# Linear attention on one core: stores of octets 0 to 7 cut into four transfers each

## The chip, the core and the metric

The kernel runs on one core of a Trainium2 chip. The metric is the device time of one execution in microseconds (us). The core has TensorE (PE, with its weight loads PEld), VectorE (DVE), ScalarE (ACT), GpSimd (POOL), SyncE (SP) and 16 DMA engines, which carry all transfers between HBM (the chip's main memory) and SBUF (the on-chip memory of 128 partitions, called rows here).

## The reference

Q, K and V have the shape batch 8, heads 12, sequence 512, dim 64 in fp32, so there are 96 heads.

```python
Q_feat = np.maximum(0, Q)
K_feat = np.maximum(0, K)
KV = np.einsum('bhkd,bhkv->bhdv', K_feat, V)
K_sum = np.sum(K_feat, axis=2)
numerator = np.einsum('bhqd,bhdv->bhqv', Q_feat, KV)
denominator = np.einsum('bhqd,bhd->bhq', Q_feat, K_sum)
return (numerator / (denominator[:, :, :, None] + 1e-10)).astype(np.float32)
```

Each input and the output have 12.58 MB.

## The kernel before

The 96 heads are worked in 12 octets of 8 heads (`NO` is 12), and K and V of an octet in two groups of 4 heads. All loads are issued ahead, in the order K, V, Q of octet 1, then of octet 2 and so on (lines 94 and 106). They come from GpSimd, because its transfers turn fp32 into bf16 on the way, and each waits for a free buffer: six octets of K and V, seven of Q. K and V of octet 0 come as fp32 through the SyncE and ScalarE queues (`k_first`, `v_first`).

For each octet the kernel prepares K (`kf`, line 138: ReLU and a mask) and V (`vo`, lines 140, 145 and 147), multiplies them on TensorE into `ps_kv` (line 152), copies the sums out to `kvd` (line 162), transposes Q (line 173) with ReLU (line 181), forms the numerator `ps_ot` (line 203) and the denominator (lines 212 to 224), transposes back (line 230) and multiplies with the reciprocal into `o_sb` (line 236). `o_sb` holds an octet's output as 128 rows of 32 x 64 fp32, 8 KB a row; a row is contiguous in the output as well, and the rows follow each other there. `outp` has `DELAY + 2` = 8 such buffers, and `k_first` and `v_first` use two of them at the start.

`store(o, o_sb)` issues the store from SyncE's queue (line 249), in octet order. The schedule is written out by hand, and a store of octet 0 to 5 also waits until the load of K of the octet six later (`k_load[o + DELAY]`) has landed; a store of a later octet waits only for its data and for what stands ahead of it in SyncE's queue. The last octet is stored in two halves of the columns (line 247). The program that comes out counts the completions of SyncE's and ScalarE's transfers on eight semaphores in turn, and a transfer waits for the earlier use of its semaphore.

Of the kernel before, what the change touches and what calls it, by code (L numbers as in the profile page):

```python
# [10 lines left out]
def kernel(  # L11
# [7 lines left out]
    nc = tc.nc  # L19
    B, H, S, D = Q.shape  # L20
    assert D == 64
    P = 128
# [5 lines left out]
    RQ = S * 8 // P  # L28
# [3 lines left out]
    NO = NG // 2  # L32
    assert NO * 8 == NH and R == 16 and RQ == 32
    DELAY = 6

    fp32 = mybir.dt.float32
    bf16 = mybir.dt.bfloat16
# [3 lines left out]
    def pool(name, bufs, **kw):  # L41
        return ctx.enter_context(tc.tile_pool(name=name, bufs=bufs, **kw))
# [6 lines left out]
    rcp = pool("rcp", 2)  # L49
    outp = pool("outp", DELAY + 2)  # L50
    otp = pool("otp", 2)
# [37 lines left out]
    k_load = {}  # L89
    after_load = mybir.DependencyInfo(mybir.DependencyClass.Sync, mybir.DependencyReason.DATA)  # L90
# [151 lines left out]
    def store(o, o_sb):  # L242
        Ov = Or[o].rearrange("p (r d) -> p r d", d=D)
        if o == NO - 1:
            for j in range(2):
                rs = slice(RQ // 2 * j, RQ // 2 * (j + 1))
                nc.sync.dma_start(out=Ov[:, rs], in_=o_sb[:, rs])
            return
        st = nc.sync.dma_start(out=Ov, in_=o_sb)
        if o + DELAY < NO:  # L250
            tc.add_manual_dep(st.ins, k_load[o + DELAY].ins.name, after_load, reason="store after load")

    def out_tile():
        return outp.tile([P, RQ, D], fp32, name="o_sb", tag="o_sb")
# [19 lines left out]
    def backs(o):  # L274
        o_sb = out_tile()
        for j in range(2):
            norm(o, j, back(o, j), o_sb)
        store(o, o_sb)
# [26 lines left out]
    o = NO - 2  # L305
# [10 lines left out]
    o_sb = out_tile()  # L316
# [4 lines left out]
    for i in range(2):  # L321
        relu_q(o + 1, i, transp(o + 1, i), nc.vector if i == 1 else None)
    norm(o, 1, ps, o_sb)
    store(o, o_sb)
    idle(5, o + 1)
    out_t(o + 1, (0,))
# [32 lines left out]
```

## Time and profile before

| what | value |
|---|---|
| time, median of 2 runs | 126.88 us (126.72 to 127.03) |
| profiled execution | 127.0 us, span 125.2 us |
| PE, DVE, ACT, POOL busy | 85.0, 81.0, 79.0, 23.7 us |
| HBM read, written | 37.75 MB, 12.58 MB |
| transfers into `out_dram` from `o_sb` | 11 of 1024 KB, 8.9 us from issue to landing (median); 2 of 512 KB, 4.5 us |
| loads of K, V and Q | 512 KB as they land, 20.5 to 21.8 us from issue to landing |
| mean granted TensorE clock | 0.950 |

The span runs from the first to the last instruction of the profiled execution; what is in its time beside the span is 1.8 us. Busy time is summed over the whole span, while the stages differ: loads alone at first, then loads and stores, then stores alone. In the view of DMA slices a digit is the busy share of the 16 DMA engines in a fortieth of the span. The bytes of a load are counted as they land, in bf16, half of what is read from HBM.

### The profile page before, as it was taken

The page shows a single profiled execution, that of the slowest core. Times are in us where ns is not written, and L with a number is a line of the kernel's source. Part 1 is how long each engine was busy: PE and PEld are TensorE (multiplying, and loading weights), DVE is VectorE, ACT ScalarE, POOL GpSimd, SP SyncE. Part 2 cuts the span into 40 slices and gives each one's busy share as a digit, 9 for nine tenths or more (in the row PEclk, how much of TensorE's full clock was granted, in tenths as well). Part 3 has the DMA queues.
Part 4 walks back from the last instruction along what each step waited for, and adds up shares of the span by engine and source line. Part 5 has one row for each costly group of instructions (what it writes and reads, how often), then busy time and mean ns, then how long its engine had stood idle before and what let it go on. Part 6 is the DMA issues. An engine that isn't in the chain of part 4 may idle for free.

```text
span 125.2 us, 2614 instructions
## 1 busy us (share of the span) xinstructions
PE 85.0 (68%) x1067; PEld 76.9 (61%) x1067; DVE 81.0 (65%) x176; ACT 79.0 (63%) x114; POOL 23.7 (19%) x40
## 2 busy tenths in 40 slices
PE   0000547898989979898966985955997597797600
PEld 0000547796878879787855983943975595775500
DVE  2006963679889797979859349449549409978610
ACT  0003737999899898989877576845499095547000
POOL 6922124221242213322121130210000000000000
PEclk9999999999999999999999599996899869999996
DMA  3999999999999999999999999999999999999991
GB/s 92 365 306 229 215 209 211 213 211 217 207 217 208 211 213 211 214 273 311 214 247 341 210 222 342 234 217 325 258 215 305 279 215 307 425 419 419 432 403 73
DMA packets 10139, 32.66 MB, mean 261 GB/s; under 512 B 784, under 2 KB 784, under 8 KB 8720
## 3 DMA queue, kind: packets, MB, share of 16 engines
q0 software_dynamic: 7712, 17.83, 74.1%
q1 hardware_dynamic: 2144, 13.63, 27.1%
q10 hardware_dynamic: 272, 1.05, 2.2%
q8 instruction: 8, 0.13, 0.4%
q14 instruction: 3, 0.02, 0.0%
HBM read 37.75 MB, written 12.58 MB: 402 GB/s over the span
## 4 chain that ended last, share of the span: by engine, by line
DVE 37%; DMA 28%; PE 19%; ACT 7%; issue 3%; DVEq 1%; ACTq 0%
DMA v_sb<-in_V_dram 20%; DVE o_sb L236 15%; PE ps_kv L152 10%; DMA k_first<-in_K_dram 7%; DVE kf L138 7%; PE ps_bk L230 7%; DVE vo L140 4%; ACT kvd L162 3%; DVE vo L147 3%; DVE den L220 2%; PE ps_qt L173 2%; DVE rec L224 2%; DVE own L215 2%; ACT qt L181 2%; ACT vo L145 1%
## 5 line engine op out<-in xcount | busy, mean ns | idle before, releaser
L152 PE MATMUL ps_kv<-vo,kf 128*128 128x132 bf16 x384 | 30.2, 240 | 19.9 <-ACT vo L145 13.8
L152 PEld LDWEIGHTS <-kf 128*128 128x128 bf16 x384 | 27.4, 107 | 21.6 <-DVE vo L140 12.9
L236 DVE TENSOR_TENSOR o_sb<-ps_bk,rec 128x1024 f32<-128x1024 f32 x24 | 28.3, 1219 | 13.6 <-PE ps_bk L230 13.6
L162 ACT CAST kvd<-ps_kv 64x260 bf16<-64x260 f32 (+1 forms) x54 | 18.6, 345 | 16.6 <-PE ps_kv L152 13.9
L205 ACT COPY ot_sb<-ps_ot 128x1024 f32<-128x1024 f32 x24 | 24.1, 1013 | 6.8 <-PE ps_ot L203 5.9
L230 PE MATMUL ps_bk<-ident,ot_sb 128*128 128x128 f32 x192 | 23.4, 276 | 0.4 <-ACT ot_sb L205 0.4
L181 ACT ACTIVATE qt<-ps_qt 128x1024 bf16<-128x1024 bf16 x23 | 22.4, 1028 | 0.2
L230 PEld LDWEIGHTS ps_bk<-ident,ot_sb 128*128 128x128 f32 x192 | 21.2, 143 | 0.7 <-ACT ot_sb L205 0.7
L203 PE MATMUL ps_ot<-qt,kvd 128*128 128x256 bf16 x96 | 14.9, 283 | 9.9 <-DVE o_sb L236 9.0
L138 DVE TENSOR_SCALAR kf<-k_sb,mask 128x1024 bf16<-128x1024 bf16 x44 | 18.4, 459 | 4.5 <-DMA k_sb<-in_K_dram 4.5
L203 PEld LDWEIGHTS <-kvd 128*128 128x128 bf16 x96 | 9.2, 100 | 13.2 <-issue 11.0
L173 PE MATMUL ps_qt<-ident,q_sb 128*128 128x128 bf16 x192 | 14.7, 237 | 0.7 <-DMA q_sb<-in_Q_dram 0.7
L173 PEld LDWEIGHTS <-q_sb 128*128 128x128 bf16 x192 | 13.3, 108 | 1.4 <-DMA q_sb<-in_Q_dram 1.3
L140 DVE TENSOR_SCALAR vo<-v_sb,mask 128x1024 bf16<-128x1024 bf16 x22 | 11.0, 501 | 4.7 <-DMA v_sb<-in_V_dram 4.7
L145 ACT ACTIVATE vo<-v_sb,mask 128x1024 bf16<-128x1024 bf16 x10 | 11.5, 1154 | 2.0 <-DMA v_sb<-in_V_dram 1.8
L94 POOL DMA_DIRECT2D v_sb<-in_V_dram x11 | 8.2, 750 | 22.2 <-DMA q_sb<-in_Q_dram 9.4
L106 POOL DMA_DIRECT2D q_sb<-in_Q_dram x12 | 7.1, 588 | 20.9 <-DMA k_sb<-in_K_dram 15.3
L94 POOL DMA_DIRECT2D k_sb<-in_K_dram x11 | 7.9, 717 | 15.4 <-DMA v_sb<-in_V_dram 9.8
L212 PEld LDWEIGHTS <-qt 128*128 128x128 bf16 x192 | 6.8, 96 | 3.6 <-ACT qt L181 2.5
L212 PE MATMUL ps_den<-kvd,qt 128*128 128x16 bf16 x192 | 7.3, 180 | 1.9 <-ACT qt L181 1.7
L145 ACT ACT_TABLE_LOAD x1 | 1.3, 1283 | 11.3 <-DMA v_first<-in_V_dram 11.3
L138 DVE TENSOR_SCALAR kf<-k_first,mask 128x1024 bf16<-128x1024 f32 x4 | 2.8, 750 | 7.7 <-DMA k_first<-in_K_dram 7.7
(24 smaller groups left out, 31.8 us busy)
## 6 DMA issues: line engine op xcount, KB each, us to landing
out_dram<-o_sb SPq DMA_DIRECT2D x11, 1024.0 KB, 8.9
q_sb<-in_Q_dram POOLq DMA_DIRECT2D x12, 512.0 KB, 20.7
k_sb<-in_K_dram POOLq DMA_DIRECT2D x11, 512.0 KB, 21.8
v_sb<-in_V_dram POOLq DMA_DIRECT2D x11, 512.0 KB, 20.5
k_first<-in_K_dram SPq DMA_DIRECT2D x1, 1024.0 KB, 9.3
v_first<-in_V_dram ACTq DMA_DIRECT2D x1, 1024.0 KB, 10.5
out_dram<-o_sb SPq DMA_DIRECT2D x2, 512.0 KB, 4.5
```

Source lines behind the costliest of these rows:

```text
L94: ld = eng.dma_start(out=t.rearrange("p g r d -> p g (r d)"), in_=X[2 * o:2 * o + 2].rearrange("g p f -> p g f"))
L138: nc.vector.tensor_scalar(kf[g][:, :, s, :], k_sb[g], scalar1=0.0, scalar2=mask[:, 0, s:s + 1], op0=Alu.max, op1=Alu.mult)
L140: nc.vector.tensor_scalar(vo[g % NB][:, :, 0, 2:D + 2], v_sb[g], scalar1=mask[:, 1, 0:1], scalar2=None, op0=Alu.mult)
L152: nc.tensor.matmul(ps_kv[:, g % 2, 0:2 * (D + 2)].rearrange("p (t d) -> p t d", t=2), kf[g][:, r, :, :].rearrange("p s d -> p (s d)"), vo[ ...
L162: copy(kvd[o % NK][64 * c:64 * c + 64, 4 * gs.start + s:4 * gs.stop:2, c * D1:c * D1 + D1].rearrange("p (g t) d -> p g t d", t=2), ps_kv[6 ...
L173: nc.tensor.transpose(ps[:, u, :], q_sb[o][:, i * (U // 2) + u, :], ident)
L181: nc.scalar.activation(to, ps, Act.Relu)
L203: nc.tensor.matmul(ps[:, i], kvd[o % NK][:, h, 1:2 * D + 1], q[:, :, h, :], start=True, stop=True, skip_group_check=True)
L205: nc.scalar.copy(ot[o][:, :, 4 * j:4 * j + 4], ps.rearrange("p h u c -> p u h c"))
L212: nc.tensor.matmul(ps[:, u], qt_sb[o % NZ][:, u, :], kvd[o % NK][:, :, 0:2 * D1:2 * D1 - 1], start=True, stop=True, skip_group_check=True)
L230: nc.tensor.transpose(ps[:, 2 * v:2 * v + 2].rearrange("p c d -> p (c d)"), ot[o][:, 8 * j + v].rearrange("p h c -> p (h c)"), ident32)
L236: nc.vector.tensor_tensor(o_sb[:, rs], ps, rec[o][:, rs].unsqueeze(2).to_broadcast([P, 16, D]), op=Alu.mult)
```

## The change

The stores of octets 0 to 7 go out in four transfers each: rows 0 to 111 in full; the right halves (4 KB) of rows 112 to 127; the left halves of the first n of these 16 rows; and the left halves of the other 16 - n. n is another number for each octet (`FIRST`). Each of the four has the same dependence on the load of K six octets later as the whole store had. Octets 8 to 11 are stored as before. What is computed and the order of all instructions on the other queues stay as they were.

```diff
+    FIRST = {0: 8, 1: 12, 2: 14, 3: 10, 4: 15, 5: 13, 6: 11, 7: 9}
...
-        st = nc.sync.dma_start(out=Ov, in_=o_sb)
-        if o + DELAY < NO:
-            tc.add_manual_dep(st.ins, k_load[o + DELAY].ins.name, after_load, reason="store after load")
+        half, a, full = RQ // 2, 112, slice(0, RQ)
+        n = FIRST.get(o)
+        if n is None:
+            parts = [(0, P, full)]
+        else:
+            parts = [(0, a, full), (a, P, slice(half, RQ)), (a, a + n, slice(0, half)), (a + n, P, slice(0, half))]
+        for lo, hi, rs in parts:
+            st = nc.sync.dma_start(out=Ov[lo:hi, rs], in_=o_sb[lo:hi, rs])
+            if o + DELAY < NO:
+                tc.add_manual_dep(st.ins, k_load[o + DELAY].ins.name, after_load, reason="store after load")
```

## The prediction

> **What bounds the kernel now.** I read the page first: the slices of the DMA engines, the queues and the HBM line.
>
> ```profile
> DMA  3999999999999999999999999999999999999991
> GB/s 92 365 306 229 215 209 211 213 211 217 207 217 208 211 213 211 214 273 311 214 247 341 210 222 342 234 217 325 258 215 305 279 215 307 425 419 419 432 403 73
> ...
> q0 software_dynamic: 7712, 17.83, 74.1%
> q1 hardware_dynamic: 2144, 13.63, 27.1%
> ...
> HBM read 37.75 MB, written 12.58 MB: 402 GB/s over the span
> ```
>
> The 16 DMA engines are busy from the second slice to the end. GB/s counts what lands: a load reads fp32 and lands bf16, so 213 is 426 on the reading side, the same as the 425 of the stores at the end. HBM moves 37.75 + 12.58 = 50.33 MB; at 425 GB/s that is 118.4 us of a 125.2 us span. No compute engine is above 68%. Second, stretches of the span:
>
> ```profile
> 10.00:50.00 40.00, 30.89 (x408) 28.64 (x409) 31.48 (x70) 33.34 (x50) 10.48 (x16) 1.00 1.10 213
> ...
> 80.00:100.00 20.00, 14.49 (x175) 12.67 (x173) 12.37 (x24) 11.47 (x17) 0.56 (x1) 0.89 1.08 263
> 100.00:107.00 7.00, 5.63 (x58) 5.12 (x57) 3.82 (x6) 5.22 (x8) 0.00 (x0) 0.82 1.08 272
> 107.00:118.00 11.00, 9.50 (x115) 8.38 (x114) 8.47 (x17) 4.87 (x10) 0.00 (x0) 1.00 1.01 425
> ```
>
> The columns are the stretch, its length, the busy time of PE, PEld, DVE, ACT and POOL, the clock, the DMA share (last but one) and GB/s. The share is 1.0 or more in every stage: loads alone until 50, loads mixed with one store per 10 us until 101, stores alone after 107. The store rate of 425 GB/s makes 1 MB 2.47 us; on 16 engines each moves 8 rows of 8 KB, 0.307 us a row and 0.154 us a half row. Third, SyncE's waits and its issues:
>
> ```profile
> SPq L249 <- DMA k_sb<-in_K_dram: 98.5, 6, 50.5
> SPq L249 <- DVE o_sb L236: 10.0, 2, 8.1
> ```
> ```profile
> 91.52 0.33 SPq L249 DMA_DIRECT2D out_dram<-o_sb  x1
> 101.75 1.86 SPq L249 DMA_DIRECT2D out_dram<-o_sb  x4
> 105.56 0.33 SPq L249 DMA_DIRECT2D out_dram<-o_sb  x1
> 114.11 0.33 SPq L249 DMA_DIRECT2D out_dram<-o_sb  x1
> 118.23 1.46 SPq L247 DMA_DIRECT2D out_dram<-o_sb  x2
> ```
>
> SyncE mostly waits, and at 101.75 it issues the stores of octets 5 to 8 at once. From there the backlog of stores never runs out: the completion records of octet 10's store (issued at 114.11) start between 119.30 and 120.65 us on the different engines, after the last store's first half was issued at 118.23. The last half completes between 121.97 and 123.55 us, mean 122.65; 1.65 us later the span ends. So the end is the slowest DMA engine's total work. The compute chain runs parallel to it from 84 us on, with about 1 us to spare at 118.23; it catches up if the DMA is relieved by more.
>
> **The change part by part.** Eight stores of one transfer become four each: 24 transfers more, the same bytes.
>
> *Issues on SyncE.* 24 x 0.333 us (an issue in the timeline) = 8.0 us of SyncE. Octets 0 to 4 are issued 10 us apart, so it costs nothing there; for octets 5 to 7 four issues take 1.33 us while one store keeps the engines busy for 2.47 us. I take 0. Without that cover it would be 3 x 3 x 0.333 = 3.0 us.
>
> *New waits on SyncE.* The changed program counts hardware transfers on eight semaphores in turn, so a transfer waits for the one eight before it. With four to a store that is the same part of the store two octets earlier. Octet 7's 112 rows wait for octet 5's, octet 8's store for octet 6's 112 rows; everything later in SyncE's order (8 to 11) queues behind. Before, these four went out together. A completion is seen some 0.37 us after its record (k_first's last record 9.67, the waiting kf at 10.04), and from issue to data it is 1.26 us (118.23 issued, first completion 120.72 less 1.23 of data): 1.63 us. Meanwhile the store in between holds the engines for 2.47 us, and the slowest are never dry. Cost 0; with the cover gone 1.63 us twice, 3.3 us. What VectorE awaits of old stores before it writes o_sb 8 to 11 had landed some 30 us earlier: 0.
>
> *Completion packets.* Each transfer writes one 4-byte completion per engine that it uses; the records show 22 ns for most. An engine in all 24 added transfers pays 0.53 us, one in only the eight right-half transfers 0.18. I take 0.35.
>
> *Uneven shares.* The 112 rows are 7 per engine and the right halves one per engine. The left halves go out as n and 16 - n rows, one row to an engine, so some engines get two and others none. If the same engines come first each time, one gets 16 left halves in place of 8 and one gets none: +1.23 to -1.23 us (8 x 0.154). If the favoured engines change from transfer to transfer it is about 0. The gain is bounded by how far the slowest engine is from the mean: 123.55 - 122.65 = 0.9 us. Between -0.9 and +1.23 I take the middle, +0.15.
>
> [...]
>
> *Other rows under each engine.* In the trace every large transfer spans 128 rows, eight to an engine, and at that all stages run at 425 GB/s: no row shows an engine waiting for another on the way out of SBUF. The 112-row transfer gives an engine seven rows, so its rows are no longer the eight that loads and stores share now, and the three small transfers have all 16 engines read within 16 neighbouring rows at one time. Lower end: an engine's rate does not depend on the row, 0 (a gain is excluded, since an engine already moves at its full rate). Upper end: each row waits for one other engine's row, 2.47 us per octet more, 19.7 in all. The nearest rows are the full-rate stores, so I stay near the lower end: one row time lost among the seven long rows, since blocks of 7 shift against blocks of 8 by at most that, and half of one among the half rows. 1.5 x 0.307 = 0.46 us per octet, 3.7 us for eight. Loads between the store's packets hide some of it in octets 0 to 4; nothing does in octets 5 to 7.
>
> [...]
>
> *Sum.* Profiled execution 127.0 us = span 125.2 + 1.8 around it; + 0.35 + 0.15 + 3.7 = 131.2 us. The two timed runs have the median 126.88, 0.1 below the profiled one; I forecast **131.1 us**. With half a row time lost per octet (1.2) and 0.2 for the rest it is 128.4; with three row times (7.4) and 1.2 it is 135.6: the likeliest case's own range.
>
> **Rivals.** *The rows don't matter* (the other side). An engine reads any row at 0.307 us; then only completions and unevenness are left: 127.0 + 0.5 = 127.5 us. For it: the full rate in stages of very different mixes, and a cost that no row of the trace shows. Against it: every one of those rows has the same eight rows per engine. It decides as soon as the loss is under 0.31 us per octet (2.5 us, 2%, over eight).
>
> *The slow engines are the relieved ones.* The shares level the 1.58 us between first and last engine: at best 0.9 us off, 126.1 us. For it: the spread exists, in two clusters; between 107.03 and 107.55 nine engines complete octet 5's store, and seven between 108.17 and 108.78. Seven 16 KB instruction packets lie before that, at about 27, 37, 48, 58, 71, 83 and 98 us, which looks like one engine each. Against it: nothing tells which engine numbers they are, and 7 late engines cannot all be the most relieved.
>
> *Full collision.* Each row waits for another: + 19.7 us, 147 us. Against: engines drift apart by 1.6 us, five row times, and so do not stay in step.
>
> *The new semaphore waits run dry.* The two waits cost 1.63 us each, 130.8 us with the small terms; it decides if a store lands over 0.8 us later than its 2.47 us. For it: they sit where no load fills in. Against: the slowest engines are behind.
>
> **How the numbers follow.** Lost row times 0.46 (0.42 of it beyond 2%, 0.04 within); full collision 0.06; waits 0.04; rows don't matter 0.26, all within 2%; levelled 0.18, 0.15 within and 0.03 for a gain beyond what I can price. Slower by over 2% (about what a measurement of this kernel can tell from no change) 0.52, within 0.45, faster 0.03. The range of 126.2 to 135.6 leaves out the full collision (0.06), the best of the levelled case (0.07) and the top of the likeliest (0.06).
>
> **What would show it.** Right: in the mixed stretches the DMA share stays at 1.0 or more while GB/s over the store's slices falls below the 340s; in the stretch of octets 5 to 7 GB/s is under 400; store packets take longer than the 0.31 us of now; loads land later. Wrong: the store-only stretch still shows about 425 GB/s and the last load lands at 107.6 us, as now. Levelling would show as completions of the last store within less than 1 us. Dry engines would show as DMA slices under 9 near 109 and 112 us.

## The result and the profile after

The changed kernel takes 128.5 us (median of 128.45 and 128.54), before 126.88 us: ratio 1.0121, 95% interval 1.0091 to 1.0151. The profiled execution has a span of 126.7 us against 125.2. It is slower, but by 1.6 us where 4.2 were forecast.

The same stretches as before; the last two columns are the DMA share and GB/s:

```profile
10.00:50.00 40.00, 30.73 (x385) 28.30 (x385) 30.45 (x69) 31.89 (x45) 10.50 (x16) 1.00 1.10 212
...
80.00:100.00 20.00, 14.62 (x183) 13.29 (x182) 12.36 (x24) 11.70 (x17) 0.56 (x1) 0.93 1.09 263
100.00:107.00 7.00, 5.76 (x63) 5.23 (x61) 3.69 (x6) 5.10 (x8) 0.00 (x0) 0.84 1.08 264
107.00:118.00 11.00, 9.50 (x115) 8.38 (x114) 8.46 (x17) 5.00 (x10) 0.00 (x0) 1.00 0.94 375
```

Up to 100 us the rate has not changed: 263 GB/s from 80 to 100 as before, although split stores lie there. From 107 to 118 us, where stores run alone, 425 GB/s have become 375 and the share has fallen from 1.01 to 0.94. Cut finer, the kernel before and then the changed one:

```profile
108.00:112.00 4.00, 4.00 (x56) 3.93 (x54) 3.28 (x8) 1.67 (x7) 0.00 (x0) 1.00 1.02 428
112.00:116.00 4.00, 2.85 (x35) 2.04 (x34) 3.24 (x6) 2.97 (x3) 0.00 (x0) 1.00 1.01 422
116.00:120.00 4.00, 1.82 (x16) 1.58 (x15) 2.36 (x2) 0.00 (x0) 0.00 (x0) 1.00 1.00 420
```
```profile
108.00:112.00 4.00, 4.00 (x57) 3.94 (x55) 3.30 (x8) 1.57 (x6) 0.00 (x0) 1.00 1.00 387
112.00:116.00 4.00, 2.85 (x36) 2.03 (x34) 3.31 (x6) 3.07 (x4) 0.00 (x0) 1.00 0.86 342
116.00:120.00 4.00, 1.95 (x16) 1.71 (x16) 2.35 (x2) 0.00 (x0) 0.00 (x0) 1.00 1.02 424
```

Two different things are to be seen. From 108 to 112 us the engines are busy all the time (1.00) and yet move only 387 GB/s in place of 428: packets take longer. In the trace's DMA records between 107.6 and 118 us, 18 of 426 packets of 8 KB take over 1.3 times the median of 0.31 us, up to 0.87 us; before it was 1 of 537. From 112 to 116 us engines also stand idle (0.86). From 116 us, with the whole stores of octets 8 to 11, all is as before.

The idle time has to do with SyncE's issues. The timeline of SyncE in the changed kernel, start and duration; from the second line on these are the last three transfers of octet 6, then octet 7's four, then octet 8's store:

```profile
103.45 0.32 SPq L258 DMA_DIRECT2D out_dram<-o_sb  x1
103.82 1.44 SPq L258 DMA_DIRECT2D out_dram<-o_sb  x1
105.30 0.99 SPq L258 DMA_DIRECT2D out_dram<-o_sb  x1
106.34 0.61 SPq L258 DMA_DIRECT2D out_dram<-o_sb  x1
108.95 0.32 SPq L258 DMA_DIRECT2D out_dram<-o_sb  x1
109.32 1.20 SPq L258 DMA_DIRECT2D out_dram<-o_sb  x1
110.56 1.38 SPq L258 DMA_DIRECT2D out_dram<-o_sb  x1
111.98 0.98 SPq L258 DMA_DIRECT2D out_dram<-o_sb  x1
113.06 0.36 SPq L258 DMA_DIRECT2D out_dram<-o_sb  x1
```

Before, the four issues in a row from 101.75 us took 0.33 to 0.44 us each. Here the first five of octets 5 and 6 (101.78 to 103.45 us) take 0.29 to 0.43, the sixth 1.44: SyncE is held, by what no record shows. The gap before 108.95 is octet 7's wait for octet 5's 112 rows, 1.9 us in the view of SyncE's waits. Octet 8's store, issued at 103.18 us before the change, now goes out at 113.06, and engines are dry (without work) before its data come.

The DMA records give the loss of the mean engine, whose last completion moved by 1.5 us, from 122.70 to 124.17. The idle time is 0.15 of 4 us, 0.6 us. What packets from 107 us on took beyond the median of their size comes to 0.6 us an engine, 0.1 before: 0.5 us more. Completion records of SyncE's queue take 0.48 us an engine over the whole run, 0.21 before. The three add up to about 1.4 us.

So four causes stood side by side: the other rows under each engine, if they are what makes packets longer (theory R; the texts below also speak of collisions or of engines that wait for each other, which no record shows as such), semaphore waits (W or S), held issues (H) and uneven shares (U). The last are in the records: followed from packet to packet, one engine takes three half rows for each of octets 5 to 7 (from 108.02 to 113.59 us), and another a single one for octet 6 (at 110.13) and for octet 7 (at 112.69). The experiments take the four apart. Each edit below is to the list `parts` of the changed kernel; an octet not named is stored whole. Times are medians, ratios against the kernel before on the same chip.

### The profile page after: what moved, and what is told of

The parts are those of the page before. It is cut to its first block, busy times and chain, and to the rows that moved or that the text cites. A ratio compares the mean times of both kernels' runs of the same rounds, so it can differ in the third digit from the quotient of the medians.

```text
span 126.7 us, 2646 instructions
## 1 busy us (share of the span) xinstructions
PE 85.3 (67%) x1067; PEld 77.7 (61%) x1067; DVE 81.3 (64%) x176; ACT 79.2 (63%) x114; POOL 23.3 (18%) x40
## 4 chain that ended last, share of the span: by engine, by line
DVE 35%; DMA 28%; PE 23%; ACT 5%; issue 2%; DVEq 1%; ACTq 0%
DMA v_sb<-in_V_dram 21%; DVE o_sb L238 15%; PE ps_kv L154 11%; DMA k_first<-in_K_dram 8%; PE ps_bk L232 6%; DVE kf L140 6%; DVE vo L142 4%; PE ps_qt L175 3%; ACT kvd L164 2%; DVE vo L149 2%; DVE den L222 2%; PE ps_ot L205 2%; DVE rec L226 2%; DVE own L217 2%; ACT qt L183 2%
## 5 line engine op out<-in xcount | busy, mean ns | idle before, releaser
L175 PE MATMUL ps_qt<-ident,q_sb 128*128 128x128 bf16 x192 | 15.7, 247 | 0.4 <-DMA q_sb<-in_Q_dram 0.4
L175 PEld LDWEIGHTS <-q_sb 128*128 128x128 bf16 x192 | 14.3, 113 | 0.9 <-DMA q_sb<-in_Q_dram 0.6
```

Of the source, the lines that this page charges most:

```text
L175: nc.tensor.transpose(ps[:, u, :], q_sb[o][:, i * (U // 2) + u, :], ident)
```

## Experiments: which octets, shares and waits cost

**e1: octets 0 to 4 alone.**

```diff
-        n = FIRST.get(o)
+        n = FIRST.get(o) if o < 5 else None
```

> Only octets 0 to 4 go out in four transfers; octets 5 to 11 go out whole, so that no store at the end waits for the one two octets earlier. Theory W (the new semaphore waits run the DMA engines dry): no slice of the DMA share under 0.95 between 107 and 118 us, time 126.3 to 127.3 us, no slower than before. Theory U (the engine that always gets two left halves has too much work): five eighths of its excess stay, about +0.9 us, 127.6 to 128.0 us, with one engine last. Theory R (other rows under each engine cost time, as forecast): five octets of eight, 127.5 us or more, with slower stores before 100 us.

Measured: 127.11 us, ratio 1.0006 (0.9998 to 1.0015). Five of the eight splits cost nothing that can be told. R as I had priced it, the same for each octet, falls here, and so does U at its full price.

**e2: the whole excess early.** (9 and 11 stand for n in octets 4 and 3.)

```diff
+        SHARE = {0: (8, 12), 1: (14, 10), 2: (15, 13), 3: (11, 16), 4: (9, 16)}
+            parts = [(0, a, full)]
+            for n, cols in zip(SHARE[o], (left, right)):
+                parts += [(a, a + n, cols)] + ([(a + n, P, cols)] if n < 16 else [])
```

> The same excess for each engine as in the change (8 half rows more on the first engine, 8 less on the sixteenth), but all of it in octets 0 to 4, by uneven right halves too; octets 5 to 11 whole, so that nothing waits at the end. Theory W: as before the change or better, 126.3 to 127.3 us. Theory U: the whole excess is there, 128.2 to 128.6 us, as the change, without a dry slice.

Measured: 127.77 us, 1.0061 (1.0049 to 1.0073): between the two theories. The last load completes at 107.84 us in place of 107.56, the last store at 123.93 in place of 123.55. So an excess of eight half rows goes with a loss of about half of U's price, and one of five, in e1, with none that can be told.

**e3: even shares, same number of transfers.**

```diff
+            parts = [(0, a, full), (a, P, slice(half, RQ)), (a, P, slice(0, half // 2)), (a, P, slice(half // 2, half))]
```

> Four transfers for each of octets 0 to 7 as in the change, with the same waits, but with the same share for all 16 engines: 112 rows, right halves, and the left halves as two groups of quarter rows. Theory W: the dry slices near 109 and 113 us are there, 127.8 to 128.6 us. Theory U: no engine has an excess; what is left is 24 completion packets on each engine, 0.5 us: 127.2 to 127.6 us.

Measured: 128.48 us, 1.0117 (1.0095 to 1.0138): as slow as the change without any unevenness. U is not the main cause. Its stretches at the end show the lost share and the lost rate together:

```profile
108.00:112.00 4.00, 4.00 (x56) 3.90 (x53) 3.27 (x8) 1.81 (x7) 0.00 (x0) 1.00 0.96 356
112.00:116.00 4.00, 2.86 (x36) 2.08 (x34) 3.09 (x6) 2.82 (x3) 0.00 (x0) 1.00 0.83 313
```

**e4: the waits alone, stores whole.**

```diff
+        parts = [(0, P, slice(0, RQ))]
+            if o in (7, 8):
+                tc.add_manual_dep(st.ins, stores[o - 2].ins.name, after_load, reason="store after store")
```

> All stores whole as before the change; the store of octet 7 waits for that of octet 5, and octet 8's for octet 6's. Theory W: dry slices near 110 and 113 us and 127.6 to 128.5 us from the waits alone. Theory U: the engines that end last never run dry, since they are behind, and the time stays at 126.6 to 127.2 us.

Measured: 127.17 us, 1.0018 (1.0007 to 1.0029). Octet 7 goes out at 109.07 and octet 8 at 111.52 us, each in 0.33 us; from 108 to 112 us the share is 0.99, and nothing is dry after that. The waits by themselves are covered, as the prediction had it, but for 0.2 us.

**e5: octets 5 to 7 alone.**

```diff
-        n = FIRST.get(o)
+        n = FIRST.get(o) if o >= 5 else None
```

> Only octets 5 to 7 go out in four transfers, octets 0 to 4 whole: the three stores that stand in SyncE's queue together. Theory H (held issues: once some five transfers stand in SyncE's queue unfetched, the issue of the next takes 1 us or more, so that a store behind three small transfers comes too late) and theory S (the semaphore waits on the store two octets earlier) both say that the whole loss is here: dry slices near 110 and 113 us, 128.2 to 128.7 us. Theory R (other rows, or uneven shares over all octets) says three eighths: 127.3 to 127.7 us.

Measured: 128.11 us, 1.0084 (1.0069 to 1.0099). With e1 this places most or all of the loss: in the three stores that are issued one behind the other at the end. Of these octet 5's still lies mostly among the last loads (before 107 us, 0.77 of its 1 MB in the kernel before). Engines run dry here too (share 0.88), with octet 8's store issued at 112.46 us:

```profile
112.00:116.00 4.00, 2.85 (x36) 2.06 (x35) 3.11 (x6) 2.84 (x3) 0.00 (x0) 1.00 0.88 345
```

## Experiments: other rows or late issues

**e6: three transfers with even shares in octets 6 and 7; no wait on a store under way.**

```diff
+        if o in (6, 7):
+            parts = [(0, a, full), (a, P, slice(half, RQ)), (a, P, slice(0, half))]
```

> Octets 6 and 7 in three transfers with even shares (112 rows, right halves and left halves of 16 rows), all others whole. By the order of the semaphores nothing between octets 5 and 9 then waits for a store that is still under way. Theory S: issues of 0.3 to 0.45 us, no dry slice, 126.8 to 127.2 us. Theory H: the last issues of octet 7 and that of octet 8 take over 1 us, a dry slice near 112 us, 127.3 to 128.2 us.

**e7: two transfers of whole rows in octets 5 to 7.**

```diff
+        if 5 <= o <= 7:
+            parts = [(0, a, full), (a, P, full)]
```

> Octets 5 to 7 in two transfers each, 112 whole rows and 16 whole rows; no semaphore wait between them. Theory S: issues of 0.3 to 0.45 us. Theory H: from about the sixth on an issue takes over 1 us, but octet 8 is issued before 109.5 us, since fewer transfers stand ahead of it, and nothing runs dry. Both: 126.8 to 127.3 us; theory R would give up to 1 us more.

Measured: e6 128.9 us, 1.0156 (1.0139 to 1.0173); e7 129.18 us, 1.0194 (1.0144 to 1.0245). Both are at least as slow as the change (the intervals just overlap), and no theory had them so. In e6 octet 8 is issued at 105.55 us and no engine is dry; neither S nor H as I had put them explains it. The stretches say what does, e6 first:

```profile
108.00:112.00 4.00, 3.40 (x51) 3.00 (x50) 3.24 (x6) 1.56 (x3) 0.00 (x0) 1.00 1.02 394
112.00:116.00 4.00, 3.45 (x43) 2.94 (x38) 2.29 (x5) 2.02 (x2) 0.00 (x0) 1.00 1.00 394
```
```profile
108.00:112.00 4.00, 3.40 (x47) 3.00 (x46) 3.24 (x6) 1.57 (x4) 0.00 (x0) 1.00 1.02 389
112.00:116.00 4.00, 3.45 (x43) 2.98 (x41) 2.29 (x5) 2.02 (x2) 0.00 (x0) 1.00 1.00 381
```

A full share with 381 to 394 GB/s: engines that count as busy while their packets take longer. In e7, 34 of 496 packets of 8 KB take over 1.3 times the median in the time from 107.6 to 118 us, the longest 1.34 us, more than four times the usual 0.31.

**e8 and e9: two transfers in octets 5 to 8, cut by columns or by rows.**

```diff
+        if 5 <= o <= 8:      # e8
+            parts = [(0, P, slice(0, half)), (0, P, slice(half, RQ))]
+        if 5 <= o <= 8:      # e9
+            parts = [(0, 64, full), (64, P, full)]
```

> Octets 5 to 8 in two transfers each, halves of the columns of all 128 rows (512 KB each). Theory H, if it is the number of transfers that counts and not their size: long issues from about the sixth on, as in the kernel with 112 and 16 rows. If only small transfers are held: 0.3 to 0.45 us each. No dry slice in either, 126.8 to 127.3 us.

> Octets 5 to 8 in two transfers each, rows 0 to 63 and rows 64 to 127, whole rows: as many transfers and bytes as with the column halves (127.4 us there), only other rows under each engine. Theory R (engines that read at one time from rows near each other wait for each other when no load packets lie between): packets of 8 KB take up to 0.62 us in place of 0.31, the stretch from 108 to 116 us falls well under 400 GB/s at a full DMA share, 129 to 137 us. Theory H (held issues) alone: 127.2 to 127.6 us, as the column halves.

Measured: e8 127.38 us, 1.0034 (1.0021 to 1.0047); e9 129.53 us, 1.0196 (1.0176 to 1.0216). As many transfers, the same bytes and octets; the rows of a transfer differ, and that is worth 2.1 us. (The packets differ too, 4 KB in e8 and 8 KB in e9, but whole stores with packets of 8 KB run at 425 GB/s.) First e8, then e9:

```profile
108.00:112.00 4.00, 3.51 (x48) 3.15 (x46) 3.24 (x8) 2.06 (x6) 0.00 (x0) 1.00 1.02 411
112.00:116.00 4.00, 3.35 (x40) 2.84 (x41) 2.37 (x5) 2.06 (x3) 0.00 (x0) 1.00 1.04 427
```
```profile
108.00:112.00 4.00, 3.50 (x48) 3.13 (x46) 3.24 (x8) 2.06 (x6) 0.00 (x0) 1.00 1.01 393
112.00:116.00 4.00, 3.36 (x40) 2.85 (x41) 2.36 (x5) 2.06 (x3) 0.00 (x0) 1.00 1.02 348
```

The full share in both leaves no idle time to explain e9. Of its packets of 8 KB between 107.6 and 118 us, 71 of 461 take over 1.3 times the median; of e8's packets of 4 and 8 KB it is 2 of 931. Why they take longer stays open: a cut by rows changes both which SBUF rows and which HBM addresses the engines work on at a time, and no run separates the two.

In e8 issues are held as well (0.94, 0.50 and 0.61 us for the sixth to eighth), with 411 and 427 GB/s. So transfers of 512 KB are held too where eight are issued in a row, while in the kernel before no issue of four in a row, of 1 MB each, took over 0.44 us; by itself that does little here.

**e10: the same two transfers of 64 rows where loads run between.**

```diff
+        if o <= 4:
+            parts = [(0, 64, full), (64, P, full)]
```

> The same two transfers of 64 rows, but for octets 0 to 4, whose stores run between loads; octets 5 to 11 whole. If load packets between the store's packets hide the waiting of the engines for each other: 126.9 to 127.6 us, loads landing as before the change. If they don't: up to 2.5 us for each of five octets, 129 us or more, and loads landing later from 60 us on.

Measured: 127.03 us, 1.0005 (0.9993 to 1.0017), and this stretch, in the kernel before and then in e10:

```profile
51.00:101.00 50.00, 39.07 (x486) 35.11 (x486) 34.13 (x68) 35.26 (x49) 6.80 (x10) 0.91 1.08 263
51.00:101.00 50.00, 38.86 (x485) 35.01 (x484) 34.10 (x68) 35.02 (x50) 6.62 (x10) 0.91 1.08 263
```

The cut that costs 2.6 us in e9 costs nothing that can be told where loads run between. The store's packets of 8 KB don't even get longer there: their mean from 51 to 101 us is 323 ns, as before. This fits e1, where octets 0 to 4 of the change cost nothing.

**e11: even shares in octets 0 to 4.**

```diff
+        if o >= 5:
+            parts = [(0, P, full)]
+        else:
+            parts = [(0, a, full), (a, P, slice(half, RQ)), (a, P, slice(0, half // 2)), (a, P, slice(half // 2, half))]
```

> Octets 0 to 4 in four transfers with the same share for all engines (112 rows, right halves, two groups of quarter rows), octets 5 to 11 whole: the kernel with uneven shares in octets 0 to 4 (127.1 us) without its unevenness. If the uneven shares relieved the engines that are late: 127.3 to 127.6 us here (15 more completion packets on each engine, 0.3 us). If they did nothing or harmed: 126.9 to 127.2 us.

**e15: uneven shares in few transfers.**

```diff
+        if o <= 2:
+            n = FIRST[o]
+            parts = [(0, a, full), (a, a + n, full), (a + n, P, full)]
```

> Uneven shares with few transfers: octets 0 to 2 as 112 rows, n whole rows and 16 - n whole rows (n = 8, 12, 14), all others whole; the first engine gets 6 half rows more, with 6 more transfers in place of 24. If uneven shares relieve the engines that end last (uneven shares in octets 0 to 4 were 0.2 us faster than even ones): 126.5 to 126.9 us, faster than before by 0.1 to 0.4%. If not: 126.9 to 127.3 us.

Measured: e11 127.3 us, 1.0025 (1.0016 to 1.0034); e15 127.24 us, 1.0016 (1.0007 to 1.0024). Against e11 the uneven shares of e1 are 0.19% faster (1.0025 less 1.0006, from runs on different occasions), and what they bring pays for the added transfers; but fewer transfers with as much unevenness are not faster than before. Whether relief reaches the engines that end last stays open; it is 0.2 us at most, and no version of it beat the kernel before.

**e12: e6 with the waits of the change.**

```diff
+            if lo == 0:
+                first[o] = st
+                if o in (7, 8):
+                    tc.add_manual_dep(st.ins, first[o - 2].ins.name, after_load, reason="store after store")
```

> The kernel with octets 6 and 7 in three transfers (128.9 us, no dry slice), and to it the waits of the change: octet 7's 112 rows wait for octet 5, octet 8's store for octet 6's 112 rows. If a dry stretch needs both the wait and the held issues behind it: a slice of the DMA share under 0.9 near 113 us, octet 8 issued after 111.5 us in place of 105.6, and 0.3 to 0.9 us more, 129.2 to 129.8 us. If the waits are covered here as they were with whole stores: 128.7 to 129.1 us.

Measured: 127.97 us, 1.0077 (1.0062 to 1.0092): 0.9 us faster than e6, where I expected it slower or the same. A short dry spell is there (share 0.99 from 108 to 112 us, octet 8 issued at 111.77), but the engines end closer together: the last half store completes from 123.24 to 124.22 us, against 122.49 to 124.98 in e6, with a mean of 123.56 against 123.33. So the mean engine lost 0.2 us and the slowest gained 0.8. That the pause let the slowest catch up fits this; no run shows it by itself.

**e13: the late issues of the change without other rows.**

```diff
+        if 5 <= o <= 7:
+            parts = [(0, P, slice(0, 26)), (0, P, slice(26, 28)), (0, P, slice(28, 30)), (0, P, slice(30, 32))]
```

> Octets 5 to 7 in four transfers each with the semaphore waits of the change, but cut by columns (26, 2, 2 and 2 of 32 columns of 256 bytes), so that every transfer has all 128 rows and the same rows under each engine as before. Theory R (the loss is engines that wait for each other over neighbouring rows): packets at their usual length, 126.9 to 127.5 us, with up to 0.4 us for completions and 512-byte packets. Theory L (the loss is late issue and dry engines): a dry slice near 113 us and 127.8 to 128.3 us, as with the transfers of the change in these octets (128.1 us).

Measured: 127.34 us, 1.0025 (1.0016 to 1.0035). SyncE waits and is held here too, but less than in e5: octet 7 goes out at 108.80 us, one small transfer is held 1.71 us, octet 8's store comes at 111.95 (112.46 in e5). Yet the share is above 1 in the stretches from 108 us on:

```profile
108.00:112.00 4.00, 3.41 (x51) 3.00 (x49) 3.24 (x6) 1.56 (x3) 0.00 (x0) 1.00 1.04 397
112.00:116.00 4.00, 3.45 (x43) 2.98 (x40) 2.29 (x5) 2.02 (x2) 0.00 (x0) 1.00 1.03 407
```

(The rate is under 425 at a share of 1.04 and 1.03; this is the run with 512-byte packets in its stores.) Waits, held issues, completions and small packets together are 0.3 us here; as many transfers cut by rows (e5) are 1.1. But the 0.8 us between them is not the rows alone, since e5 runs dry and e13 does not. Ordered by the issue of octet 8's store, the share from 112 to 116 us in the runs with both the waits and held issues is 1.00 at 111.77 us (e12), 1.03 at 111.95 (e13), 0.88 at 112.46 (e5), 0.86 at 113.06 (the change) and 0.83 at 113.73 (e3). The cuts differ in these runs too, but up to 111.95 us the late issue leaves engines busy, and from 112.46 on it does not. So e13 stays just on the covered side and so does not give the price of the dry time in the change.

**e14: 96 and 32 rows in place of 112 and 16.**

```diff
-        a, full = 112, slice(0, RQ)      # as e7, octets 5 to 7
+        a, full = 96, slice(0, RQ)
```

> Octets 5 to 7 in two transfers of whole rows, 96 and 32, beside 112 and 16 (129.2 us). If the number of neighbouring rows that all 16 engines read at once sets the waiting: fewer engines meet in 32 rows than in 16, the longest packets of 8 KB stay under 0.9 us in place of 1.3, and the time is 127.5 to 128.7 us. If any departure from 128 rows costs the same: 129.0 to 129.4 us.

Measured: 129.13 us, 1.0161 (1.0143 to 1.018), the longest packet 1.27 us. The first expectation missed, the second held: with 32 rows in the small transfer in place of 16 the time is 129.13 us against 129.18 (e7), no difference that can be told. How the longer packets depend on the cut stays open.

## Why the prediction was wrong, and where it was right

*What bounds the kernel*: right for the kernel before. The engines' total work sets the end, and the time follows what happens after 101 us; e1, e5 and e10 show that only this stage counts. The changed kernel also has idle time there.

*Other rows under each engine*: the step that failed, by its size. The effect is there (e8 against e9, and e7 with packets of up to four times the length), and 0.46 us per octet was of the right order, if too low, for the row cuts in few transfers: e9 loses 2.6 us in four octets, e7 2.2 in three, e6 1.9 in two. But I charged it for all eight octets, 3.7 us. Five of them run between loads, and there it is nothing that can be told (e1, e10). In the change itself the longer packets are 0.5 us of the mean engine in all. The prediction had the sentence that loads between the packets hide some of it in octets 0 to 4, and did not take it into the sum: three octets at 0.46 us would have been 1.4, and the forecast 128.8 us. That this comes near the 128.5 measured would still be partly luck, since idle time, which I put at 0, makes up as much of the loss as the longer packets.

Where stores run alone at the end, a cut by rows slows them and one by columns, which keeps all 128 rows, does not (348 and 427 GB/s from 112 to 116 us, e9 and e8); what about the rows does it isn't shown.

*Issues on SyncE*: the duration was wrong, up to 1.44 us in place of 0.333, from the sixth of the issues that begin at 101.78 us on; the cost of 0 is nearly right for held issues by themselves: e8, with three of them and no wait, is 0.4 us slower in all.

*New waits*: the cover was counted for issues of 0.33 us. With held issues behind the wait, engines do run dry (share 0.86 from 112 to 116 us). So a second term failed: put at 0, the two together cost 0.6 us of the mean engine in the change. The sign that I named for that rival showed, but its price of 3.3 us did not: 0.2 us for the waits alone (e4), 0.3 where late issues stay covered (e13), 0.6 where they don't.

*Completion packets* of 0.35 us fit e11: 15 more on every engine, 0.3 us. *Uneven shares* of +0.15 us: between e1 (nothing) and e2 (0.8 us, with nearly as many transfers as the change has in all and all unevenness early), not better known.

Of the rivals, "the rows don't matter" is refuted by e9, with the HBM addresses as the part of the cut that no run separates; levelling brought at most 0.2 us (the mean of the last completions before is 122.70, not 122.65, so the room for it was 0.85 us); full collision stayed far off, at 0.95 us per octet in the worst cut (e6) in place of 2.47.

## What to carry to other kernels

A store cut by rows can slow the DMA engines at a share of 1.0, since longer packets count as busy: 348 GB/s at a share of 1.02 (e9), where the cut by columns had 427 at 1.04 (e8). Read GB/s beside the share, stage by stage, and try such a cut by columns first. Before a cost per transfer is multiplied, sort the transfers by what runs beside them; here it cost nothing that can be told beside load packets (1.0006 in e1, 1.0005 in e10). And count the transfers in a queue, not only the bytes: in the change, semaphores that are used in turn and issues of up to 1.44 us moved octet 8's store by 10 us (103.18 to 113.06) and left the mean engine idle for 0.6 us.

## What the runs showed of the hardware that I had not expected

- Stores cut into 64 + 64 rows lose nothing that can be told between loads (e10, 1.0005) and 0.64 us per store of 1 MB at the end (e9).
- With the same waits, no engine ran dry where octet 8's store was issued at 111.95 us, and engines did at 112.46 us (shares 1.03 and 0.88 from 112 to 116 us, e13 and e5).
- Of the issues that follow each other on SyncE from 101.8 us on, in the change and in e13, the first five took 0.29 to 0.49 us and the sixth 1.44 and 0.97; the longest was 2.2 us (e3, the last small group of octet 6). Whole column halves were held too (0.94 us in e8), and with the 64-row transfers of e9 it was the third that took 1.45 us. What is counted stays open.
- A wait made the stage of stores alone faster: 128.9 to 127.97 us (e6, e12), with the engines' last completions 1.0 us apart in place of 2.5.
